# Out-projection of a three-branch flow step: token tiles in pairs, seven half-size products in place of eight

## The chip, the cores and the metric

The kernel runs on one core of a Trainium2 chip. The metric is device time in microseconds (us) of one launch. Engines are called as the profile calls them: PE (TensorE, matrix products), DVE (VectorE), ACT (ScalarE), POOL (GpSimd) and SP (SyncE, which issues most DMA transfers). PE writes its products to banks of PSUM; DVE and ACT read them there; POOL works on SBUF alone.

## What is computed

A layer of a flow model works on 2,048 sample tokens and 128 prompt tokens of width 1,024. An input projection feeds three token mixers; their outputs are projected, gated and summed into `merged`. What the change touches is the end:

```python
merged = jnp.einsum('btnd,btnd->btd', gt, pb)
out = jnp.einsum('btd,de->bte', merged, w_out)
h = h + gate * out
y = rmsnorm(h, final_g)
```

All tensors are float32. The kernel carries each operand of a large product as two float16 parts, hi and lo, and forms hi·hi + hi·lo + lo·hi, three products for one.

## The kernel before

The launch is one long program; a scheduler sets the order of the instructions on each engine by dependences and by priority (code under `tc.high_priority()` goes ahead of what could run beside it), and each engine then works strictly through its own list. The part before the change is the third merge (branch n = 0): `merge` goes through eight blocks `db` of 128 output columns. In each block PE forms, for five spans of tokens (four of 512 columns, one of 128), 24 products for the sigmoid gate (`gemm_T` with the kept input `xh`, `xl`) and 12 for the branch projection; ACT takes the sigmoid (L1389), DVE multiplies (L1398), POOL adds to the row `mrow` (L1399), and POOL's queue writes the row to the DRAM tensor `mrg` (L1406). The weights of later blocks are loaded to the two buffers `wst`, scaled and split beside this. In every block `tail` calls `out_w`, which loads one eighth of W_out, measures it and splits it into `whi`, `wlo` (names `wohi`, `wolo` in the trace).

The scale of a tensor comes from `scales` (L183 to L187): the sums of squares of 128 partitions are cast (L175), added up by a one-column product with a tile of ones on PE, and three short DVE operations turn the result into a power of two. The one-column product of an out-projection tile is the row `b<-mscb,ones`.

The out-projection goes through 17 tiles of 128 tokens, in the order 16 (the prompt), 8 to 15, 0 to 7. `out_prep` loads a tile of `mrg` (L1455), squares it on ACT (L1464), gets its scale, and splits it (L1466 on ACT for hi, L1467 on DVE for lo), all from L1464 on under high priority. It is called for the first five tiles before the last half of the last merge block (`ahead_out`), and then for tile i + 5 while tile i is worked on. PE forms 24 products of 128x512 for each half of the output (`gemm_N`). DVE multiplies with the gate (L1524), POOL adds the residual rows (L1525), ACT squares (L1534), DVE and POOL make the inverse root (L170, L171), DVE scales (L1537), and SP issues the store (L1538).

## Time and profile before

| | |
|---|---|
| median of 3 runs | 2188.82 us (2185.91 to 2192.23) |
| the profiled execution | 2189.41 us, span 2187.6 us |
| PE busy | 2123.6 us, 97% of the span |
| DVE, ACT, POOL busy | 60%, 46%, 32% |
| mean granted PE clock | 0.991 |
| last merge ends, last product of the out-projection | 2001.4, 2179.8 |

PE is the engine that sets the time; what matters of the others is where PE waits for them. In the views a time such as 2004.05 is microseconds from the start of the span. A row `x128` counts instructions; the mean of one product is longer than the distance between two, because products overlap in the array. In a view of stretches, PEclk is the granted clock as a share of full speed.

### The profile page before, as it was taken

What the parts mean: (1) busy time and instruction counts of PE and PEld (TensorE: products, weight loads), DVE (VectorE), ACT (ScalarE), POOL (GpSimd) and SP (SyncE); (2) the same over time, 40 slices, a digit from 0 to 9 for tenths busy, and PEclk for the clock granted to TensorE, in tenths of its full rate; (3) what the DMA queues carried; (4) which work ended last, traced back from release to release, by engine and by line L of the source; (5) the groups of instructions that cost most, each with busy time, mean ns of one, the idle gap of its engine ahead of it and who ended that gap; (6) DMA issues with size and microseconds to landing.
All of it is one profiled execution on the core that took longest, in us unless ns stands there. A gap on an engine that the chain in (4) does not pass through costs nothing.

```text
span 2187.6 us, 42676 instructions
## 1 busy us (share of the span) xinstructions
PE 2123.6 (97%) x16234; PEld 1214.9 (56%) x16234; DVE 1320.9 (60%) x3150; ACT 1015.0 (46%) x2355; POOL 701.6 (32%) x862
## 2 busy tenths in 40 slices
PE   7999999999999998999899999999999999999998
PEld 3565444455555587878555556555554444444443
DVE  5746854469879698776665555765663544323454
ACT  3644744345566474554544445655543422222332
POOL 1421333223334324322312223344432221222543
PEclk9999999999999999999999999999999999999999
DMA  8424823167777664544655555766654544324542
GB/s 282 141 87 148 290 95 106 61 204 222 253 232 240 198 197 139 146 121 127 197 183 157 174 160 180 242 196 203 198 173 150 174 129 129 116 78 127 173 148 103
DMA packets 304727, 365.09 MB, mean 167 GB/s; under 512 B 39585, under 2 KB 215946, under 8 KB 302474
## 3 DMA queue, kind: packets, MB, share of 16 engines
q1 hardware_dynamic: 289386, 302.19, 45.4%
q0 software_dynamic: 12688, 51.27, 6.5%
q10 hardware_dynamic: 2448, 8.91, 1.0%
q8 instruction: 127, 2.08, 0.4%
q14 instruction: 78, 0.64, 0.1%
HBM read 234.67 MB, written 127.62 MB: 166 GB/s over the span
## 4 chain that ended last, share of the span: by engine, by line
PE 50%; DMA 4%; DVE 4%; ACT 1%; issue 1%; POOL 0%; SPq 0%; DVEq 0%; POOLq 0%; ACTq 0%
PE b L161 50%; DMA st<-br 1%; DMA ES<-ei 1%; DMA mrg<-mrow 1%; DMA wst<-in_w_in_dram 0%; DVE XB L797 0%; DVE E L798 0%; DVE big L1360 0%; DMA mrow<-mrg 0%; DMA S<-in_state_delta_dram 0%; DMA wst<-in_w_branch_dram 0%; PE b L1057 0%; ACT big L1359 0%; DMA sq__2210_18514<-qT 0%; DMA qk<-n 0%
## 5 line engine op out<-in xcount | busy, mean ns | idle before, releaser
L161 PE MATMUL b<-xh,whi 128*128 128x512 f16 (+1 forms) x1920 | 652.6, 349 | 1.4 <-DVE mrow L1395 1.0
L161 PE MATMUL b<-xl,whi 128*128 128x512 f16 (+1 forms) x1920 | 652.9, 349 | 0.0
L161 PE MATMUL b<-xh,wlo 128*128 128x512 f16 (+1 forms) x1920 | 651.6, 348 | 0.0
L161 PEld LDWEIGHTS <-whi 128*128 128x128 f16 x3904 | 358.1, 98 | 329.2 <-issue 10.2
L161 PEld LDWEIGHTS <-wlo 128*128 128x128 f16 x1952 | 191.6, 98 | 179.0 <-issue 3.6
L161 PE MATMUL b<-big,bhi 128*128 128x512 f16 (+1 forms) x960 | 249.7, 347 | 1.4 <-ACT big L1359 1.1
L1399 POOL TENSOR_TENSOR mrow<-mrow,sg 128x512 f32<-128x512 f32 (+1 forms) x80 | 92.6, 1158 | 282.9 <-DVE sg L1398 220.5
L161 PE MATMUL b<-big,blo 128*128 128x512 f16 (+1 forms) x480 | 163.1, 347 | 0.0
L1389 ACT ACTIVATE sg<-b,winv 128x512 f32<-128x512 f32 (+1 forms) x120 | 74.2, 618 | 172.0 <-PE b L161 171.1
L161 PEld LDWEIGHTS <-xh 128*128 128x128 f16 x1496 | 117.7, 98 | 28.0
L161 PEld LDWEIGHTS <-bhi 128*128 128x128 f16 x960 | 86.9, 98 | 75.6
L1398 DVE SCALAR_TENSOR_TENSOR sg<-b,binv,sg 128x512 f32<-128x512 f32 (+1 forms) x80 | 53.4, 667 | 121.4 <-PE b L161 118.7
L646 POOL TENSOR_TENSOR cy<-cy,raw 128x545 f32<-128x545 f32 (+1 forms) x48 | 66.4, 1408 | 185.7 <-ACT raw L645 185.7
L175 DVE CAST wscb<-wss 128x1 bf16<-128x1 f32 x93 | 14.3, 154 | 154.5 <-ACT wlo L209 71.4
L866 POOL COPY T<-ES 32x256 f16<-32x256 f16 x68 | 31.0, 456 | 220.1 <-DMA ES<-ei 217.6
L161 PE MATMUL b<-whi,xh 128*128 128x128 f16 x544 | 94.0, 220 | 0.0
L161 PE MATMUL b<-wlo,xh 128*128 128x128 f16 x544 | 93.9, 220 | 0.0
L161 PE MATMUL b<-whi,xl 128*128 128x128 f16 x544 | 93.8, 220 | 0.0
L161 PE MATMUL b<-wohi,mh 128*128 128x512 f16 x240 | 90.9, 379 | 1.3 <-ACT mh L1466 1.3
L161 PE MATMUL b<-wohi,ml 128*128 128x512 f16 x240 | 90.8, 379 | 0.3 <-DVE mscb L175 0.3
L161 PE MATMUL b<-wolo,mh 128*128 128x512 f16 x240 | 90.9, 379 | 0.0
L209 ACT ACTIVATE wlo<-wst 128x1024 f16<-128x1024 f32 x52 | 54.9, 1056 | 77.4 <-DMA wst<-in_w_in_dram 75.5
(456 smaller groups left out, 4298.1 us busy)
## 6 DMA issues: line engine op xcount, KB each, us to landing
wst<-in_w_in_dram SPq DMA_DIRECT2D x60, 512.0 KB
qkv<-cy POOLq DMA_DIRECT2D x12, 1089.0 KB, 5.2
st<-br SPq DMA_DIRECT2D x48, 256.0 KB
mrow<-mrg SPq DMA_DIRECT2D x18, 512.0 KB
mrow<-mrg SPq DMA_DIRECT2D x16, 576.0 KB
mrg<-mrow POOLq DMA_DIRECT2D x16, 576.0 KB, 3.6
dc<-dec SPq DMA_DIRECT2D x17, 512.0 KB
kq<-qkv SPq DMA_DIRECT2D x34, 256.0 KB
```

What stands on the lines that cost most here:

```text
L161: PE.matmul(out, l, r, start=start, stop=stop)
L175: V.tensor_copy(sb16, ss)
L209: A.activation(w.lo, st, AF.Square, accum_out=ss)
L646: G.tensor_tensor(y[:, c0:c1], y[:, c0:c1], raw[:, 1 + c0:1 + c1], ALU.mult)
L866: G.tensor_copy(T16[rows(a0, b), :, :, b], ES[0:32, :, 2 * a0 + b, :, wT])
L1389: A.activation(sg, ps, AF.Sigmoid, scale=gw.inv)
L1398: V.scalar_tensor_tensor(sg, ps, binv[:, 1:2], sg, ALU.mult, ALU.mult)
L1399: G.tensor_tensor(mr, mr, sg, ALU.add)
```

## The change

The 16 sample tiles are taken in eight pairs. A pair of tiles (a above b) times W_out is a product of 2 x 2 blocks: four blocks of 128 tokens x 512 channels on one side and four quarters of W_out (512 x 512) on the other. Instead of eight block products the kernel forms seven, of sums and differences of the blocks (Strassen's scheme in the form with few additions). Tile 16 stays single.

- Four sums of W_out quarters are made in blocks 3 to 6 of the last merge (`out_pair`), split into hi and lo, and written to a DRAM tensor `tw` of 4.19 MB; after the merge they are loaded over `xh`, which has no reader left. All of W_out has one scale now, measured in blocks 0 to 2 (`out_squares`), so W_out is read twice.
- For each pair POOL makes four sums of the blocks of a and b (`pair_sums`), one scale is taken for both tiles (`m_scale`), and `pair_operands` splits seven operands, with ACT for hi and DVE for lo, into the place of `xl`. Only the splitting stands under high priority.
- Each product (`formed`) is 12 matrix products of 128x512 in one bank. The seven are joined by ACT copies (`kept`), DVE additions (`joined`) and POOL additions, then gated and added as before.
- The operands of pair i + 1 are prepared at the end of the code of pair i; only tile 16 and the sums of the first pair are prepared ahead.

```diff
+    def out_squares(i):
+        st = read_w(w_out[0][:, i * P:(i + 1) * P], KT)
+        A.activation(sb(orp, [P, KT, P], "t16", F16, bufs=2), st, AF.Square, accum_out=wos[:, i:i + 1])
+
+    def out_pair(j):
...
+        left, right = [read_w(w_out[0][:, i * P:(i + 1) * P], KT) for i in (j, j + 4)]
+        for i, st in ((j, left), (j + 4, right)):
+            hi, lo = [w_[:, :, i * P:(i + 1) * P] for w_ in (whi, wlo)]
+            A.activation(hi, st, AF.Copy, scale=s)
+            V.scalar_tensor_tensor(lo, st, s, hi, ALU.mult, ALU.subtract)
...
+            G.tensor_tensor(tf, x_, y_, op_)
+            t16 = sb(orp, [P, 2, 4, P], "t16", F16, bufs=2)
+            A.activation(t16[:, 0], tf, AF.Copy, scale=s)
+            V.scalar_tensor_tensor(t16[:, 1], tf, s, t16[:, 0], ALU.mult, ALU.subtract)
+            SY.dma_start(twD[:, n, j], t16.rearrange("p l k c -> p (l k c)"))
...
+    def m_scale(mts):
...
+            A.activation(jk, mt, AF.Square, accum_out=ss[:, i:i + 1])
...
+        s, inv = scales(ss[:, 2:3] if len(mts) > 1 else ss[:, 0:1], orp, "msc")
...
+    def pair_sums(ts, pl, tag):
+        a, b = [m_load(t, pl, tag) for t in ts]
+        s, minv = m_scale([a, b])
...
+        G.tensor_tensor(sf[:, 0], a21, a22, ALU.add)
+        G.tensor_tensor(sf[:, 1], sf[:, 0], a11, ALU.subtract)
+        G.tensor_tensor(sf[:, 2], a11, a21, ALU.subtract)
+        G.tensor_tensor(sf[:, 3], a12, sf[:, 1], ALU.subtract)
...
+        with tc.high_priority():
+            halved(v[:, 0, 0:2].rearrange("p s k c -> p (s k) c"), v[:, 1, 0:2].rearrange("p s k c -> p (s k) c"), a, s)
+            halved(v[:, 0, 2], v[:, 1, 2], b[:, 4:8], s)
+            halved(v[:, 0, 3:7], v[:, 1, 3:7], sf, s)
...
-            for i, t in enumerate(order[:5]):
-                pre.append(out_prep(t, *((wp, "wst") if i % 3 else (big, "mrow")), None if i < 3 else wp))
+            pre.append(out_single(16))
+            pre.append(pair_sums(PAIRS[0], wp, "wst"))
...
+    for n in (2, 0, 1, 3):
+        SY.dma_start(tw[:, n].rearrange("p j l k c -> p j (l k c)"), twD[:, n])
+    nxt = pair_operands(0, *pre[1])
...
+        def formed(slot, w, even):
+            ps = bank(ps_mm if even else ps_d, [P, 512])
+            for k in range(4):
+                mm(ps, v[:, 0, slot, k, :], w(0, k), k == 0, False)
+                mm(ps, v[:, 0, slot, k, :], w(1, k), False, False)
+                mm(ps, v[:, 1, slot, k, :], w(0, k), False, k == 3)
+            return ps
...
+        u1 = kept(formed(0, raw(0, 0), True))
+        u2 = joined(temp(), formed(4, mixed(2), False), u1)
+        c11 = joined(u1, formed(1, raw(1, 0), True), u1)
...
+        u5 = kept(formed(3, mixed(0), False))
+        u3 = joined(temp(), formed(5, mixed(1), True), u2)
+        G.tensor_tensor(u2, u2, u5, ALU.add)
+        G.tensor_tensor(u5, u3, u5, ALU.add)
...
+        c12 = joined(u2, formed(6, raw(1, 1), False), u2)
...
+        c21 = joined(u3, formed(2, mixed(3), True), u3)
...
+        if not end:
+            nxt = pair_operands(i_ + 1, *pair_sums(PAIRS[i_ + 1], op, "mt"))
```

Where the instructions stand is shown at three places. On PE before, in the middle of a tile of the out-projection (`wohi`, `wolo` are W_out, `mh`, `ml` the tile, `b` a PSUM bank, `mscb` the cast sums of squares of a tile five places later):

```order
L161 MATMUL b_26086<-wohi_23213,mh_25695 128x512
L161 LDWEIGHTS ones_2_89
L161 MATMUL b_25867<-mscb_25868,ones_2_89 128x1
L161 LDWEIGHTS mh_25695
L161 MATMUL b_26086<-wolo_23214,mh_25695 128x512
L161 LDWEIGHTS ml_25696
L161 MATMUL b_26086<-wohi_23213,ml_25696 128x512
```

On PE in the changed kernel, where the second pair ends and the third begins (`xh` holds the sums of W_out quarters, `xl` the seven operands; `b_25854` is the pair's last product, `mscb` belongs to the third pair, whose products begin with `b_25912` and `b_25942`):

```order
L161 MATMUL b_25854<-xh_93,xl_94 128x512
L161 LDWEIGHTS ones_2_89
L161 MATMUL b_25885<-mscb_25886,ones_2_89 128x1
L161 LDWEIGHTS xl_94
L161 MATMUL b_25912<-wohi_23213,xl_94 128x512
L161 LDWEIGHTS xl_94
L161 MATMUL b_25912<-wolo_23214,xl_94 128x512
L161 LDWEIGHTS xl_94
L161 MATMUL b_25942<-wohi_23213,xl_94 128x512
```

The one-column product has moved from between the products of other, earlier tiles to the seam between two pairs, directly ahead of the products that need its scale.

On DVE before, around the same one-column product `b_25867` (`inv` is the gate's factor, `ml` the lo part):

```order
L1524 TENSOR_TENSOR hh_26056<-b_26059,gt_26057 128x512
L183 COPY msc_25871<-b_25867 128x1
L185 TENSOR_SCALAR msc_25871<-msc_25871 128x1
L186 TENSOR_SCALAR msc_25871<-msc_25871 128x1
L187 TENSOR_SCALAR msc_25871<-msc_25871 128x1
L1469 TENSOR_SCALAR inv_3224_25878<-winv_2810_23215,msc_25871 128x8
L1467 SCALAR_TENSOR_TENSOR ml_25864<-mt_25861,msc_25871,mh_25863 128x1024
```

On DVE in the changed kernel, at the same seam (`sg_25813` is the block that the last product `b_25854` completes, `hss` the inverse root of the finished rows `hh`, `xl` the lo operands of the third pair, `sf` the sums that POOL made):

```order
L1631 TENSOR_TENSOR sg_25813<-b_25854,sg_25813 128x512
L183 COPY msc_25889<-b_25885 128x1
L1607 SCALAR_TENSOR_TENSOR sg_25813<-sg_25813,minv_25734,gb_25522 128x512
L185 TENSOR_SCALAR msc_25889<-msc_25889 128x1
L170 TENSOR_SCALAR hss_25848<-hss_25848 128x1
L186 TENSOR_SCALAR msc_25889<-msc_25889 128x1
L187 TENSOR_SCALAR msc_25889<-msc_25889 128x1
L1489 TENSOR_TENSOR minv_25894<-msc_25889,osc_24076 128x1
L1494 SCALAR_TENSOR_TENSOR xl_94<-mt_25876,msc_25889,xl_94 128x1024
L1577 SCALAR_TENSOR_TENSOR hh_25747<-hh_25747,hss_25848,fg_25524 128x1024
L1494 SCALAR_TENSOR_TENSOR xl_94<-mt_25878,msc_25889,xl_94 128x512
L1494 SCALAR_TENSOR_TENSOR xl_94<-sf_25896,msc_25889,xl_94 128x2048
```

The scale (L183 to L186) now stands among the operations that join and gate the last product, and the splitting follows it.

On SP in the changed kernel, at the end of the merge (`mrow` and `wst` from `mrg` with 8x128 are tile 16 and the first pair, `mt` the second pair; before, five tiles were loaded at this place and nothing as large as `tw`):

```order
L1477 DMA mrow_25369<-mrg 128x8x128
L1477 DMA wst_25389<-mrg 128x8x128
L1477 DMA wst_25391<-mrg 128x8x128
L1377 DMA mrow_25418<-mrg 128x1024
L1553 DMA xh_93<-tw 128x4096 x4
L1559 DMA hh_25520<-in_x_prompt_dram 128x1024
L1564 DMA gb_25522<-gate 128x1024
L1566 DMA fg_25524<-in_final_g_dram 128x1024
L1559 DMA hh_25587<-in_x_sample_dram 128x1024
L1559 DMA hh_25589<-in_x_sample_dram 128x1024
L1477 DMA mt_25716<-mrg 128x8x128
L1477 DMA mt_25718<-mrg 128x8x128
```

The four loads of `tw` stand ahead of the residual rows and of the second pair's tiles.

More of the change, by code (lines that the diff above doesn't have):

```diff
@@ L1507, in hybrid_flow_kernel @@
     SY.dma_start(fg, final_g[None, :].to_broadcast([P, D]))
[L1509 to L1529 removed]
+    jk = sb(op, [P, D], "ojk", F16, bufs=1)
```

160 lines of the change are left out of this document (105 added, 55 removed).

## Prediction

> **What bounds the kernel now.** I read the busy shares first, then the stretch of the out-projection, then the chain that ended last there, then the groups of the same stretch for durations.
>
> ```profile
> core 0: us, PE busy (x) PEld busy (x) DVE busy (x) ACT busy (x) POOL busy (x), PEclk, DMA share, GB/s
> 2004.00:2092.00 88.00, 87.97 (x415) 40.04 (x416) 45.00 (x94) 27.36 (x39) 44.02 (x36) 1.00 0.53 172
> ```
>
> ```profile
> 2004.05 175.78 PE b L161 x826
> ```
>
> PE has no gap in this stretch, its clock is full, and it carries the chain for 175.8 us. DVE, ACT and POOL are half idle or more. So products taken away are worth their full distance, and every moment in which PE waits costs its full length. The distance between two products is read from two starts, eleven apart:
>
> ```profile
> 2177.06 0.38 PE L161 MATMUL b<-wohi,mh 128*128 128x512 f16 x1
> ...
> 2179.43 0.38 PE L161 MATMUL b<-wohi,ml 128*128 128x512 f16 x1
> ```
>
> 2.37 us / 11 = 0.2155 us.
>
> **Products removed.** A pair had 2 x 48 products and has 7 x 12 = 84. Eight pairs save 96 x 0.2155 = **20.7 us**. Tile 16 is unchanged.
>
> **End of the merge.**
>
> ```profile
> 1998.19 1.06 ACT L1464 ACTIVATE ml<-wst 128x1024 f16<-128x1024 f32 x1 [0.71 <-DMA wst<-mrg]
> ...
> 1999.89 1.06 ACT L1464 ACTIVATE wlo<-mrow 128x1024 f16<-128x1024 f32 x1 [0.55 <-DMA mrow<-mrg]
> ...
> 2001.51 1.14 ACT L1466 ACTIVATE mh<-mrow,msc 128x1024 f16<-128x1024 f32 x1
> ...
> 2002.69 1.28 DVE L1467 SCALAR_TENSOR_TENSOR ml<-mrow,msc,mh 128x1024 f16<-128x1024 f32 x1 [0.23 <-ACT mh L1466]
> ```
>
> Before, tile 16's hi waits behind a fourth square that now isn't there (three tiles are loaded ahead, not five). Hi can start at 2000.1, after the third square and the last sigmoid (0.7), lo at 2001.3, and PE goes on at 2002.6, not 2004.05: **-1.4 us**. The first pair's operands: POOL's block sums and row additions from 1998.2 on (five by 1.27 us, row below) end at 2004.6, ACT's hi of 28 blocks of 128 columns (1.15 us for eight, as the row above) at 2007.9 and DVE's lo of the last 16 at 2010.5; PE has done tile 16 at 2002.6 + 44 x 0.2155 = 2012.1. So nothing waits there.
>
> **The seam between two pairs.** The durations (each row ends its first part with busy time and mean ns of one):
>
> ```profile
> L1525 POOL TENSOR_TENSOR hh<-hh,xr 128x512 f32<-128x512 f32 x30 | 38.0, 1267 | 74.0 <-DVE hh L1524 44.8 <-issue 24.6 <-DVE msc L187 4.5
> L1524 DVE TENSOR_TENSOR hh<-b,gt 128x512 f32<-128x512 f32 x32 | 22.0, 687 | 26.0 <-PE b L161 22.8 <-POOL gt L1489 3.0 <-DMA out_dram<-hh 0.2
> L1467 DVE SCALAR_TENSOR_TENSOR ml<-mt,msc,mh 128x1024 f16<-128x1024 f32 x12 | 15.4, 1283 | 3.0 <-ACT mh L1466 3.0
> L1464 ACT ACTIVATE ml<-mt 128x1024 f16<-128x1024 f32 x12 | 12.7, 1057 | 36.4 <-PE b L161 27.0 <-POOL hh L1525 7.4 <-DMA mt<-mrg 2.0
> L171 POOL TENSOR_TENSOR hss<-hss,mhalf 128x1 f32<-128x1 f32 x17 | 9.3, 550 | 1.8 <-DVE hss L170 1.8
> L1537 DVE SCALAR_TENSOR_TENSOR hh<-hh,hss,fg 128x512 f32<-128x512 f32 x2 | 1.4, 749 | 0.7 <-POOL hss L171 0.7
> ```
>
> The way from scale to hi, in order of time:
>
> ```profile
> 2004.20 0.15 DVE L185 TENSOR_SCALAR msc<-msc 128x1 int32<-128x1 int32 x1
> 2004.39 0.15 DVE L186 TENSOR_SCALAR msc<-msc 128x1 int32<-128x1 int32 x1
> ...
> 2004.57 1.15 ACT L1466 ACTIVATE mh<-wst,msc 128x1024 f16<-128x1024 f32 x1 [1.92 <-DVE msc L186]
> ```
>
> Preparing the next pair is not under high priority up to its scale, so PE's list has the one-column product behind the last product of the running pair, and the first products of the next pair right behind it. Nothing is left on PE to cover the way from scale to operands. From the end of the last product (0): DVE joins its bank (0.04 to 0.72), copies the scale (0.08 more until the next start), gates the block (L1607, two SBUF operands, as the 749 ns row: 0.82 to 1.57), then L185, a short L170 and L186 (1.57 to 1.91, the second start 0.19 after the first as in the rows); ACT splits tile a for hi (1.94 to 3.09). PE restarts at **3.1**. It can do four hi products (0.86), then waits for lo: DVE 3.13 to 4.41, PE at 4.48, another **0.5**. The other operands (hi by 6.1, lo by 9.0) are ready before PE reaches them at 8.8. L170 needs ACT's square of the finished rows, which needs POOL's addition (done 0.2 after the end, square 1.4): no further delay. So a seam costs **3.6 us** of waiting; bounds: 2.4 without the join and the gate in front of the scale, 4.6 if POOL slows a DVE operation by 1 us. That is for five seams. At the sixth of the seven, DVE's list has two gate operations between copy and L186: 4.5.
>
> The first seam is longer. The second pair's tiles are loaded behind `tw` and five transfers of 0.52 MB. Loads ran here at:
>
> ```profile
> 2016.00:2022.00 6.00, 6.00 (x29) 2.71 (x28) 2.08 (x6) 1.15 (x1) 2.22 (x2) 1.00 0.90 263
> ```
>
> Before, tiles of 0.524 MB landed 1.70 us apart at the merge's end (the two ACT rows above that waited for DMA), 308 GB/s. `tw` can start when PE has read `xh` for the last time, at 1999: 4.19 + 3.67 MB then take 30 us at 263 GB/s, 25.5 at 308, and the second tile lands at 2029 or 2025. (`tw` itself comes in time: its first quarter is there by 2004, and used at 2014.7.) The first pair's products end at 2012.1 + 84 x 0.2155 = 2030.2. From the landing on, POOL makes three block sums (ACT's two squares and `kept`, 2 x 1.06 + 0.7, end within them), a join, a sum and a join (6 x 1.27 = 7.6); DVE gates that result (0.75), joins the last block (0.69), and comes to L186 after 1.2 as above; ACT's hi takes 1.15: 11.4 us together. PE restarts at 2036.4 to 2040.4, 6.2 to 10.2 us late, and 0.5 for lo. I take **8**, between the two.
> Seams together: 5 x 3.6 + 4.5 + 8 = **30.5 us**.
> Inside a pair the change adds a wait on ACT: the square of the next pair's second tile stands ahead of the first `kept`. That tile's buffer comes free with DVE's lo at 4.4 and its load needs some 4 us (row under the merge's blocks); PE needs the bank that `kept` empties at the seventh product, 72 x 0.2155 = 15.5 us after its start. No cost.
>
> **PE's clock.** What did idle stretches of this size do to it? Pairs of rows: an idle stretch, then 3.4 us shortly behind it.
>
> ```profile
> 603.88:606.28 2.40, 0.00 (x0) 0.03 (x1) 2.31 (x5) 2.40 (x12) 0.45 (x1) 1.00 0.87 236
> 606.97:610.38 3.41, 3.41 (x13) 1.39 (x11) 3.38 (x9) 3.41 (x16) 2.94 (x3) 0.51 1.03 363
> 1056.88:1059.70 2.82, 0.00 (x1) 0.03 (x1) 1.61 (x6) 2.47 (x6) 1.03 (x2) 1.00 1.00 379
> 1060.99:1064.40 3.41, 3.33 (x39) 3.17 (x37) 3.24 (x11) 1.79 (x6) 0.15 (x1) 0.50 0.40 107
> 1539.90:1541.66 1.76, 0.00 (x1) 0.00 (x0) 0.38 (x4) 1.10 (x3) 0.00 (x0) 1.00 1.05 369
> 1542.27:1545.68 3.41, 3.27 (x16) 1.88 (x17) 2.90 (x7) 0.56 (x1) 0.26 (x1) 0.50 0.20 58
> 2001.40:2002.70 1.30, 0.01 (x2) 0.00 (x0) 0.83 (x3) 1.25 (x2) 0.41 (x1) 1.00 0.00 0
> 2002.70:2006.10 3.40, 3.11 (x15) 1.40 (x16) 2.41 (x8) 1.15 (x1) 0.00 (x0) 1.00 0.29 61
> ```
>
> ```profile
> 708.31:710.11 1.80, 0.01 (x1) 0.00 (x0) 1.80 (x3) 1.80 (x4) 0.00 (x0) 1.00 0.01 2
> 710.80:714.20 3.40, 2.97 (x49) 2.71 (x47) 3.40 (x11) 2.65 (x6) 2.93 (x4) 1.00 0.82 176
> ```
>
> Idle for 1.76, 2.40 and 2.82 us, then half clock for 3.41 us; idle for 1.30 and once for 1.80 us, no drop. Seams of 3.1 us are beyond all of these, so I count one half-clock stretch each, 3.41 / 2 = 1.7 us: 7 x 1.7 = **11.9 us** (bounds 0, and 23.8 for two each).
> [...]
>
> **The last merge's blocks.** Squares, splits and POOL sums cost nothing by themselves: 4 x 36 products of 0.2155 us and the short span cover 33 us in each block, and blocks 3 to 6 add some 6 us to each of ACT, DVE and POOL. But the next weights go to the same two buffers, and PE stands at their one-column products. A load takes 3.7 us to use, and L1398 takes 0.75:
>
> ```profile
> L1398 DVE SCALAR_TENSOR_TENSOR sg<-b,binv,sg 128x512 f32<-128x512 f32 x32 | 24.0, 750 | 101.9 <-PE b L161 99.4 <-ACT sg L1389 2.0 <-issue 0.3
> ```
>
> ```profile
> 1845.49 0.37 SPq L195 DMA_DIRECT2D wst<-in_w_out_dram  x1
> ...
> 1849.19 1.06 ACT L209 ACTIVATE wolo<-wst 128x1024 f16<-128x1024 f32 x1 [1.02 <-DMA wst<-in_w_out_dram]
> ```
>
> In block 4 the second W_out tile gets its buffer 3.4 us into the block and lands at 7.1; DVE ends that tile's lo at 9.5 (1.15 + 1.28) and L1398 at 10.3, POOL a row addition at 11.6 and its second sum at 12.9, which frees the buffer; the branch weights are there at 16.6 and measured and cast at 17.6. PE stands at their product after 72 long and 16 short products, at 16.4: 1.2 us late; by the same working 0.9 in block 5 and none in 3 and 6. I take **+2.0** (0 to 8: 2 us in each of the four), short enough to leave the clock.
>
> **The tail.**
>
> ```profile
> 2179.85 0.69 DVE L1524 TENSOR_TENSOR hh<-b,gt 128x512 f32<-128x512 f32 x1 [3.62 <-PE b L161]
> ...
> 2183.21 1.41 DVE L1537 SCALAR_TENSOR_TENSOR hh<-hh,hss,fg 128x512 f32<-128x512 f32 x2 [0.66 <-POOL hss L171]
> ```
>
> Before, the last scaling starts 3.4 us after the last product. Now DVE has two joins, two gates, a further gate and an addition of 0.7 each (to 3.9), then the other tile's full scaling, which waits for POOL's root (to 6.1), then sum, root (0.55) and scaling at 7.1: **+3.7 us**.
>
> **Sum:** -20.7 + 30.5 + 11.9 - 1.4 + 2.0 + 3.7 = **+26.0 us**. The profiled execution took 2189.41 us with a span of 2187.6, 0.6 above the median; on the median of 2188.8 the forecast is **2214.8 us**. A measurement can tell about 0.3% (6.6 us) from no change.
>
> **Rivals.**
> - *The clock stays full*: the four hi products inside each seam count as activity, and no drop follows. Everything else stands: 2214.8 - 11.9 = 2202.9 us. For it, the 1.80 us gap that had no drop; against it, three drops at gaps shorter than a seam. Chance 0.18. [...]
> - *Longer seams*: POOL, busy with sums at each seam, slows a DVE operation there (+1 us x 7), the first seam takes 11 (+3), all four merge blocks wait (+6): 2230.8 us. For it, one of DVE's scalings took a microsecond more than the others while POOL worked:
>
> ```profile
> 2042.85 2.28 DVE L1537 SCALAR_TENSOR_TENSOR hh<-hh,hss,fg 128x1024 f32<-128x1024 f32 x1 [0.41 <-POOL hss L171]
> ...
> 2052.41 1.28 DVE L1537 SCALAR_TENSOR_TENSOR hh<-hh,hss,fg 128x1024 f32<-128x1024 f32 x1 [1.03 <-POOL hss L171]
> ```
>
> Against it, most such rows show no increase. Chance 0.13.
> - *Short seams*: 2.4 us of waiting at six of them (14.4), 8 at the first, full clock: -20.7 + 22.4 - 1.4 + 2.0 + 3.7 = +6.0, 2194.8 us, no change. Chance 0.05.
> - *Faster: the one-column product runs early.* If PE took it while the pair's products run, the scale, hi and lo would be ready at the seam: six seams at 0, the first at 2: -20.7 + 2 - 1.4 + 2.0 + 3.7 = -14.4, 2174.4 us. The point from which it decides: -20.7 - 1.4 + 2.0 + 3.7 = -16.4, so seams that cost under 16.4 / 7 = 2.3 us each, clock included, make the kernel faster, under 1.4 us by more than 0.3%. Against it, DVE's cast below was ready to run at 1997.5 and waited for PE, which had not yet read the cast before it, since that product kept its place among the merge's products:
>
> ```profile
> 1997.30 0.19 ACT L1464 ACTIVATION_READ_ACCUMULATOR ml<-wst 128x1 f32 x1
> ...
> 1998.71 0.16 DVE L175 CAST mscb<-mss 128x1 bf16<-128x1 f32 x1 [2.85 <-PE b L161]
> ```
>
> Chance 0.06. That the change doesn't do what it says can be left aside: the order shows 84 products a pair.
>
> **How the numbers follow.** Forecast 0.58. The low end, 2198, is the full clock with no wait in the merge and a first seam of 6 (2202.9 - 2 - 2, rounded down); the high end, 2232, is the longer-seams case. Below lie short and early seams (0.11), above some of the rest. Slower by over 0.3% (above 2195.4): 0.58 + 0.18 + 0.13 = 0.89, less 0.02 for errors common to all cases, 0.87; within 0.3%: 0.05 and one of these, 0.06; faster: 0.07.
>
> **What would show it.** Right: in the new profile PE idles seven times, each time until ACT's hi (L1493) and then DVE's lo (L1494), 3 us and 0.5 us, with PEclk 0.5 behind each; products of the out-projection number 720; the last L1577 starts 7 us after the last product. Wrong: PE busy through the seams, or a drop of the clock at no seam, or PE waits of over 2 us in a merge block.

## The result, and the profile after

The changed kernel takes **2244.51 us** (median of 6 runs, 2242.13 to 2248.70), the kernel before 2188.61 us on the same chip (6 runs, 2185.91 to 2193.03): a ratio of 1.0253, 95% interval 1.0237 to 1.0268. The forecast was 2214.8 us, 2198 to 2232. The sign is right; the size is not, by 30 us, and the time lies outside the range. The profiled execution took 2242.51 us with a span of 2240.7.

I cut the span into four stages at instructions that all kernels here have: up to the one-column product ahead of the last merge's first block; the merge, up to the one-column product that stands directly behind its last product (that of the tile or pair after tile 16); the out-projection, up to the last product's end; the tail.

| us | start of the merge | merge | out-projection | tail | span |
|---|---|---|---|---|---|
| before | 1732.9 | 268.4 | 178.6 | 7.8 | 2187.6 |
| after | 1728.3 | 294.7 | 204.5 | 13.1 | 2240.7 |
| difference | -4.6 | **+26.3** | +26.0 | +5.3 | +53.1 |

The first stage is not touched by the change. It ended between 1726 and 1743 us in the 19 profiled executions of this study, so kernels that differ by a few us are compared by stage below, and only times of several runs by their medians.

The stretch of the merge, before and then after (columns as in the prediction: length, busy time of PE, PEld, DVE, ACT, POOL, granted clock, DMA share, GB/s):

```profile
1732.80:2001.20 268.40, 268.40 (x1473) 129.79 (x1473) 90.48 (x255) 70.12 (x115) 54.24 (x58) 1.00 0.36 112
```

```profile
1728.30:2023.10 294.80, 275.28 (x1468) 132.59 (x1467) 103.51 (x233) 80.61 (x129) 80.70 (x74) 0.97 0.42 132
...
2026.00:2114.00 88.00, 72.97 (x315) 31.36 (x314) 56.04 (x80) 33.55 (x46) 52.65 (x42) 0.92 0.54 183
```

The merge had no gap on PE before. Now PE is idle for 19.5 us in it and the clock is at 0.97. The last row answers to the stretch of the out-projection that the prediction starts from: 73 us of PE's work in 88 us, at 0.92 of the clock. What PE waited for (total us, times, longest), first over the whole kernel, the longest total, then in the merge (1728 to 2026 us):

```profile
PE b L161 <- ACT xl L1493: 32.1, 7, 7.5
```

```profile
PE b L161 <- DVE wscb L175: 12.2, 4, 5.8
PE b L161 <- ACT sg L1389: 4.5, 2, 3.9
PE b L161 <- DVE sg L1398: 2.8, 2, 2.0
```

The first row is the seven seams between pairs: 32.1 us, and the forecast said 30.5. The other three, 19.5 us together, hardly exist in the prediction. `wscb` is the scale of the next block's weights; the sigmoid (L1389) and the multiplication (L1398) empty PE's banks.

**A merge block.** Block 4 in order of time, on SP, ACT, DVE and PE (start, length, what; idle time before it and who ended it):

```profile
1874.14 0.38 SPq L195 DMA_DIRECT2D wst<-in_w_out_dram  x1
1874.79 0.39 PE L161 MATMUL b<-xh,whi 128*128 128x512 f16 x1
1877.78 1.15 ACT L1463 ACTIVATE wohi<-wst,osc 128x1024 f16<-128x1024 f32 x1 [5.28 <-DMA wst<-in_w_out_dram]
1878.96 1.28 DVE L1464 SCALAR_TENSOR_TENSOR wolo<-wst,osc,wohi 128x1024 f16<-128x1024 f32 x1 [4.85 <-ACT wohi L1463]
1882.76 1.28 DVE L223 SCALAR_TENSOR_TENSOR wlo<-wst,wsc,whi 128x1024 f16<-128x1024 f32 x1 [0.49 <-ACT whi L222]
1884.08 0.38 SPq L195 DMA_DIRECT2D wst<-in_w_out_dram  x1
1889.29 1.15 ACT L1463 ACTIVATE wohi<-wst,osc 128x1024 f16<-128x1024 f32 x1 [5.99 <-DMA wst<-in_w_out_dram]
1890.48 1.31 DVE L1464 SCALAR_TENSOR_TENSOR wolo<-wst,osc,wohi 128x1024 f16<-128x1024 f32 x1 [6.43 <-ACT wohi L1463]
1891.71 0.74 DVE L1398 SCALAR_TENSOR_TENSOR sg<-b,binv,sg 128x512 f32<-128x512 f32 x1
1892.50 0.22 PE L161 MATMUL b<-xh,whi 128*128 128x128 f16 x1 [2.00 <-DVE sg L1398]
1895.48 0.38 SPq L195 DMA_DIRECT2D wst<-in_w_branch_dram  x1
1899.14 0.16 DVE L175 CAST wscb<-wss 128x1 bf16<-128x1 f32 x1 [2.15 <-ACT blo L209]
1899.35 0.16 PE L161 MATMUL b<-wscb,ones 128*128 128x1 bf16 x1 [5.79 <-DVE wscb L175]
```

Read it from the second W_out load (1884.08). It is issued 9.3 us into the block, because its buffer is freed by DVE's `wlo` (1882.76), which waits for ACT, whose list held the split of the first W_out tile ahead of it and stood 5.28 us at that tile's transfer. The second tile makes ACT and DVE stand again (5.99 and 6.43 us), and L1398, which only has to empty a bank, stands in DVE's list behind that tile's lo: PE idles 2.00 us. The branch weights get a buffer at 1895.48, and PE idles 5.79 us at their scale. The same in block 1 with the squares: ACT stood 6.67 us at a tile to be squared, with a sigmoid behind it, and PE idled 3.86.

**The clock.** Idle stretches and the half clock behind them, in the merge and at a seam:

```profile
1893.55:1899.36 5.81, 0.02 (x2) 0.01 (x1) 0.97 (x3) 2.27 (x5) 3.16 (x3) 0.56 0.39 135
1894.24:1904.48 10.24, 5.13 (x29) 3.21 (x29) 5.29 (x14) 4.44 (x8) 6.38 (x6) 0.50 0.29 98
...
2081.17:2084.90 3.73, 0.00 (x1) 0.00 (x1) 2.11 (x9) 2.35 (x4) 3.73 (x3) 1.00 0.00 0
2085.39:2088.80 3.41, 3.41 (x9) 0.94 (x8) 2.97 (x4) 3.00 (x4) 1.24 (x1) 0.50 0.37 104
```

In the merge the clock was half for 17.1 us, 5.3 of them while PE stood anyway: half of the rest, 5.9 us, is lost, since products started 0.426 us apart at 0.50 of the clock (1788.43 to 1791.41) and 0.2155 at full. In the out-projection it was half for 30.7 us, 4.4 of them idle: 13.1 lost.

**A seam**, the second one:

```profile
2081.01 0.17 PE L161 MATMUL b<-mscb,ones 128*128 128x1 bf16 x1
2081.21 0.69 DVE L1631 TENSOR_TENSOR sg<-b,sg 128x512 f32<-128x512 f32 x1
2081.82 0.15 DVE L183 COPY msc<-b 128x1 f32<-128x1 f32 x1
2081.93 0.85 DVE L1607 SCALAR_TENSOR_TENSOR sg<-sg,minv,gb 128x512 f32<-128x512 f32 x1
2082.27 1.06 ACT L1572 ACTIVATE ojk<-hh 128x1024 f16<-128x1024 f32 x1 [7.38 <-POOL hh L1610]
...
2083.45 0.15 DVE L170 TENSOR_SCALAR hss<-hss 128x1 f32<-128x1 f32 x1 [0.60 <-ACT ojk L1572]
2083.52 0.14 DVE L186 TENSOR_SCALAR msc<-msc 128x1 int32<-128x1 int32 x1
...
2083.70 1.76 ACT L1493 ACTIVATE xl<-mt,msc 128x1024 f16<-128x1024 f32 x2 [0.28 <-DVE msc L186]
...
2084.90 0.39 PE L161 MATMUL b<-wohi,xl 128*128 128x512 f16 x1 [3.73 <-ACT xl L1493]
```

The order is the one forecast: one-column product last, join, scale, gate, the scale's last step, hi. One wait was denied in the prediction and is there: L170 stands 0.60 us at ACT's square of finished rows.

**The tail**, on DVE, from PE's last product on:

```profile
2227.25 0.69 DVE L1631 TENSOR_TENSOR sg<-b,sg 128x512 f32<-128x512 f32 x1 [1.54 <-PE b L161]
2227.98 1.72 DVE L1607 SCALAR_TENSOR_TENSOR sg<-sg,minv,gb 128x512 f32<-128x512 f32 x2
...
2230.33 1.03 DVE L1607 SCALAR_TENSOR_TENSOR sg<-sg,minv,gb 128x512 f32<-128x512 f32 x1
2231.40 1.64 DVE L1610 TENSOR_TENSOR hh<-sg,hh 128x512 f32<-128x512 f32 x1
...
2235.97 1.41 DVE L1577 SCALAR_TENSOR_TENSOR hh<-hh,hss,fg 128x512 f32<-128x512 f32 x2 [0.66 <-POOL hss L171]
```

The last scaling starts 8.4 us after PE's end; 7.1 was forecast.

### The profile page after: what moved, and what is told of

Its sections match the earlier page's. It is cut to its first block, busy times and chain, and to the rows that moved or that the text cites. A ratio compares the mean times of both kernels' runs of the same rounds, so it can differ in the third digit from the quotient of the medians.

```text
span 2240.7 us, 42539 instructions
## 1 busy us (share of the span) xinstructions
PE 2118.0 (95%) x16123; PEld 1208.8 (54%) x16123; DVE 1371.2 (61%) x3124; ACT 1043.5 (47%) x2395; POOL 784.0 (35%) x908
## 5 line engine op out<-in xcount | busy, mean ns | idle before, releaser
L161 PEld LDWEIGHTS <-whi 128*128 128x128 f16 x3840 | 352.2, 98 | 330.2 <-issue 18.1
L161 PEld LDWEIGHTS <-xl 128*128 128x128 f16 x1488 | 141.5, 100 | 137.6 <-ACT xl L1493 34.1
L1399 POOL TENSOR_TENSOR mrow<-mrow,sg 128x512 f32<-128x512 f32 (+1 forms) x80 | 98.0, 1225 | 252.7 <-DVE sg L1398 183.5
L1389 ACT ACTIVATE sg<-b,winv 128x512 f32<-128x512 f32 (+1 forms) x120 | 74.0, 617 | 139.1 <-PE b L161 138.4
L646 POOL TENSOR_TENSOR cy<-cy,raw 128x545 f32<-128x545 f32 (+1 forms) x48 | 75.3, 1596 | 181.2 <-ACT raw L645 181.2
L1398 DVE SCALAR_TENSOR_TENSOR sg<-b,binv,sg 128x512 f32<-128x512 f32 (+1 forms) x80 | 53.3, 666 | 104.1 <-PE b L161 96.6
L161 PE MATMUL b<-wohi,xl 128*128 128x512 f16 x192 | 68.6, 428 | 32.7 <-ACT xl L1493 32.1
L175 DVE CAST wscb<-wss 128x1 bf16<-128x1 f32 x85 | 13.0, 153 | 134.7 <-ACT wlo L209 81.0
L223 DVE SCALAR_TENSOR_TENSOR wlo<-wst,wsc,whi 128x1024 f16<-128x1024 f32 x52 | 71.5, 1379 | 32.2 <-ACT whi L222 32.1
```

Source lines behind the costliest of these rows:

```text
L161: PE.matmul(out, l, r, start=start, stop=stop)
L175: V.tensor_copy(sb16, ss)
L223: V.scalar_tensor_tensor(w.lo, st, s, w.hi, ALU.mult, ALU.subtract)
L646: G.tensor_tensor(y[:, c0:c1], y[:, c0:c1], raw[:, 1 + c0:1 + c1], ALU.mult)
L1389: A.activation(sg, ps, AF.Sigmoid, scale=gw.inv)
L1398: V.scalar_tensor_tensor(sg, ps, binv[:, 1:2], sg, ALU.mult, ALU.mult)
```

## The experiments

Stages of each version, one profiled execution each (medians of several runs stand in the text where there are any; nosq, nosum, calm0, seam4, held, noadd and final2 ran once):

| us | start of the merge | merge | out-projection | tail | span |
|---|---|---|---|---|---|
| mergeonly | 1732.8 | 294.9 | 181.6 | 7.8 | 2217.2 |
| nosq | 1732.3 | 285.6 | 205.4 | 13.1 | 2236.4 |
| nosum | 1731.8 | 281.2 | 206.0 | 13.5 | 2232.6 |
| own | 1738.8 | 276.1 | 206.8 | 13.1 | 2234.8 |
| calm | 1736.8 | 267.9 | 204.4 | 10.6 | 2219.8 |
| calm0 | 1737.7 | 268.3 | 204.5 | 10.7 | 2221.1 |
| fill | 1735.7 | 292.9 | 198.9 | 13.1 | 2240.6 |
| seam | 1739.8 | 295.4 | 183.7 | 11.4 | 2230.2 |
| seam4 | 1736.2 | 293.4 | 180.1 | 15.2 | 2224.9 |
| held | 1737.9 | 296.2 | 170.3 | 13.3 | 2217.7 |
| noadd | 1735.2 | 296.7 | 177.5 | 9.6 | 2219.0 |
| best | 1742.8 | 278.1 | 179.9 | 18.1 | 2218.9 |
| final | 1735.7 | 269.5 | 170.2 | 13.4 | 2188.7 |
| final2 | 1734.7 | 267.9 | 169.5 | 16.4 | 2188.5 |
| final3 | 1733.8 | 267.9 | 172.0 | 15.8 | 2189.5 |
| final4 | 1738.7 | 267.9 | 170.1 | 14.4 | 2191.1 |
| final5 | 1725.7 | 268.3 | 178.4 | 13.2 | 2185.5 |

### The merge

**mergeonly**: the new merge with the out-projection of before (its `out_w` replaced by the two functions of the change, as they are).

```diff
-    def out_w(i):
-        w = load_w(w_out[0][:, i * P:(i + 1) * P], KT, hi=whi[:, :, i * P:(i + 1) * P], lo=wlo[:, :, i * P:(i + 1) * P])
...
+    def out_squares(i):
...
+    def out_pair(j):
...
+            V.tensor_copy(winv, wsc[1].to_broadcast([P, KT]))
```

> The changed kernel's last merge (one scale, squares, splits, quarter sums and their stores) with the out-projection of before (17 single tiles, eight products of quarters; the stored sums are not read). Theory A, the loss sits in the merge's blocks: the merge again takes some 294 us instead of 268, all behind it as before, 2188.6 + 26.4 = 2215 us (2208 to 2220). Rival B, the merge is late only because of the new preparation at its end (two tiles and pair sums instead of five tiles), or the loss sits in the out-projection: within 6 us of before, 2183 to 2195.

Measured: 2223.07 us (2218.97 to 2227.16, 2 runs) beside 2189.28 before; merge 294.9 us. The merge's 26 us are there without the pairs, and all of them: theory A, though the total lies 3 us above its range. (The out-projection takes 3 us more than before: PE waits 2.7 us for tile 16's hi part, with a half clock behind it.)

**nosq** and **nosum** take one kind of added work out of the merge.

```diff
 (nosq)
-            for i in range(3 * db, min(3 * db + 3, KT)):
-                out_squares(i)
+            if db == 0:
+                V.memset(wos[:, 0:KT], 1.0)
```

> The changed kernel without the eight squares of W_out's tiles and their eight loads in the first three blocks of the merge; the scale comes from a constant that gives the same power of two. Theory A (each wait in the merge belongs to one kind of tile in flight): PE's waits in the second block (2.3 and 3.9 us) and the half clock behind them (3.4 us, 1.7 lost) go, and those of the later blocks (12 us, 6.8 lost) stay: the merge takes 294.7 - 8 = 287 us (284 to 290). Rival B, waits only move: without the squares the later blocks wait longer, merge 292 us or more. Whole kernel about 2237 us.

```diff
 (nosum)
-            G.tensor_tensor(tf, x_, y_, op_)
-            t16 = sb(orp, [P, 2, 4, P], "t16", F16, bufs=2)
...
+        for n in range(4):
+            SY.dma_start(twD[:, n, j], zero)
```

> The changed kernel with the four quarter sums of each pair of W_out tiles and their splits left out (zeros are stored in their place, so the products with them are wrong); squares, loads and splits of W_out stay on the two shared buffers. Theory A (a W_out tile's buffer is late because of the in-order lists at its loads and splits): about half of the waits in blocks 4 to 6 (12 us and 6.8 us of clock) stay, since the second W_out tile is still loaded late and the next weights behind it; merge 294.7 - 8 = 287 us (282 to 291). Rival B, POOL's sums alone hold the buffers: the waits from block 4 on all go, merge 294.7 - 19 = 276 us or less.

Measured: without the squares 285.6 us (9.1 less), without the sums 281.2 (13.5 less). PE's idle stretches of block 1 went with the squares (11.7 us are left of 19.5), as theory A says for nosq. nosum lies between its two theories, outside both ranges and a little nearer to B (276) than to A (287): the sums hold the buffers for a good part, not alone. The two gains add up to 22.6 of the 26.3 us. Neither settles whether it is the work or the waiting for tiles.

**own**: the same work, W_out's tiles in a buffer that the merge's weights don't use.

```diff
+    LOADS = [(0, 1), (2, 3), (4, 5), (6, 7)] + [(j, j + 4) for j in range(4)]
+    def read_two():
+        st = sb(orp, [P, 4, 4, P], "sf").rearrange("p s k c -> p (s k) c")
...
-        left, right = [read_w(w_out[0][:, i * P:(i + 1) * P], KT) for i in (j, j + 4)]
+        left, right = two
```

> The changed kernel with W_out's tiles staged in the buffer of the pair sums, which is not yet in use, two tiles at a time and one pair of tiles ahead, instead of in the two buffers that the merge's weights use. Theory A, the merge loses its 26.4 us because W_out's tiles and the merge's weights wait for each other in two shared buffers, and ACT's and DVE's lists stand behind a tile in flight: PE's idle stretches of over 0.6 us in the merge go and with them the half clock, 2244.5 - 26 = 2218 us (2213 to 2224). Rival B, ACT, DVE and POOL are too busy with the added squares, splits and sums, whatever the buffers: at least 2235 us.

Measured: merge 276.1 us, so 18.6 of the 26.3 us go with a buffer of its own and the earlier loads that it allows; 2237.50 us (2236.59 to 2238.42, 2 runs) in all, which by its total is rival B. By its merge it is nearer to A: in the profiled execution the merge began late (1738.8). Some 4 us of that are the edit's own: ahead of the merge ACT stands 3.3 us at the first W_out tile and 3.2 us at a tile of the next weights, a sigmoid stands behind, and PE idles 2.1 us for it, with a half clock after; the rest lies within the spread of the start. What is left in the merge are two idle stretches of 2.9 and 2.8 us. The first is again a list that stands at a tile:

```profile
1877.52 1.01 SPq L1458 DMA_DIRECT2D sf<-in_w_out_dram  x2
...
1882.76 1.29 DVE L1476 SCALAR_TENSOR_TENSOR wolo<-sf,osc,wohi 128x1024 f16<-128x1024 f32 x1 [2.92 <-ACT wohi L1475]
...
1884.62 1.63 DVE L1476 SCALAR_TENSOR_TENSOR wolo<-sf,osc,wohi 128x1024 f16<-128x1024 f32 x1
1886.17 0.20 DVE L175 CAST wscb<-wss 128x1 bf16<-128x1 f32 x2
```

The tiles are asked for only when the last sums have freed the buffer, DVE's lo stands at them, and the cast (L175) that PE waits for comes behind both tiles' lo. The second stretch has another cause: L1398, at 1899.22, stands behind the lo of a sum of W_out quarters, which waits 2.13 us for ACT, and ACT waits 3.29 us for POOL's sum; the four sums of a tile pair go through one buffer (`tf`).

**calm** and **calm0**: the same splits, sums and stores, but a scale for each pair of column tiles (8 loads in place of 16), the separate buffer, and the four pairs spread over blocks 1, 3, 5 and 6; in calm they are also held back by a value of the running block.

```diff
+    def out_pair(j, one):
+        left, right = two
+        for i, st in enumerate(two):
+            A.activation(sb(orp, [P, KT, P], "t16", F16, bufs=2), st, AF.Square, scale=one, accum_out=wos[:, i:i + 1])
...
+        if j < 3:
+            read_two(j + 1)
...
+            one = sb(orp, [P, 1], "one")
+            V.tensor_scalar(one, sg[:, 0:1], 0.0, 1.0, ALU.mult, ALU.add)
```

> The changed kernel with another preparation of W_out: one scale for each pair of column tiles instead of one for all (so no squares ahead: 8 tile loads, not 16; the scales' inverses go into the gate rows), the pair of tiles staged in the pair sums' buffer, its load a block or more ahead, and its squares, splits and sums held back by a value of the running block's first sigmoid, so that ACT and DVE never stand at a tile in flight. The same splits, sums and stores as in the changed kernel. Theory A, the merge's 26 us come from lists that stand at tiles in flight, not from the work: merge 268.4 + 0 to 6 us (after: 294.7), whole kernel 2244.5 - 23 = 2221 us (2217 to 2227). Rival B, the added work by itself crowds ACT, DVE and POOL: merge 280 us or more.

```diff
 (calm0, against calm)
-            A.activation(sb(orp, [P, KT, P], "t16", F16, bufs=2), st, AF.Square, scale=one, accum_out=wos[:, i:i + 1])
+            A.activation(sb(orp, [P, KT, P], "t16", F16, bufs=2), st, AF.Square, accum_out=wos[:, i:i + 1])
```

> As the kernel whose merge lost nothing (267.9 us; one scale for each pair of column tiles, own staging buffer, held back by a value of the block's first sigmoid), but not held back: squares, splits and sums stand where the scheduler puts them, right behind the loads. Theory A, what cost the time is that ACT's and DVE's lists stand at tiles in flight: PE waits again in the merge, 274 us or more. Rival B, the eight loads left out and the separate buffer are enough: merge 272 us or less, as with the hold.

Measured: calm 2217.86 us (2214.14 to 2221.58, 2 runs), merge 267.9 us; calm0 268.3. The merge's stretch in calm:

```profile
1736.90:2004.90 268.00, 268.00 (x1471) 129.89 (x1470) 104.03 (x252) 84.15 (x140) 82.91 (x73) 1.00 0.41 129
```

Set it beside after's row: DVE, ACT and POOL do as much work (104.03, 84.15 and 82.91 us; after 103.51, 80.61 and 80.70), PE has no gap, the clock is full, and all 26.3 us are gone. So the work itself costs nothing; rival B is out. But my narrower theory is out too: without the holding back nothing comes back. In calm0 ACT did stand at W_out's tiles in the merge, and PE had no gap:

```profile
ACT t L1464 <- DMA sf<-in_w_out_dram: 15.6, 6, 3.5
```

In calm ACT stood at none, in the changed kernel 35.4 us (18.3 at tiles to be split, 17.1 at tiles to be squared), but in the kernel before, too, 17.6 us, six times, without a gap on PE. So a list that stands at a tile is not by itself the cost; it is where the buffer of the next weights, or the emptying of a bank, comes too late by it. What is shown is that the cost hangs on where the tiles are staged and how often they are loaded (own: 18.6 us by the buffer and its earlier loads; the rest goes with the halved loads and the wider spacing, which I did not take apart).

### The clock and the seams

**fill**: unused products in the seams.

```diff
-            nxt = pair_operands(i_ + 1, *pair_sums(PAIRS[i_ + 1], op, "mt"))
+            ab = pair_sums(PAIRS[i_ + 1], op, "mt")
+            ps = bank(ps_x, [P, 512])
+            for _ in range({0: 30, 5: 20}.get(i_, 12)):
+                mm(ps, v[:, 0, 2, 0, :], whi[:, 0, 0:512])
+            nxt = pair_operands(i_ + 1, *ab)
```

> The changed kernel with products that nothing uses put in each seam behind the one-column product: 12 of 128x512 (2.6 us), 30 in the first seam, 20 in the sixth; they end before the next pair's operands are ready, so no seam gets longer. Theory A, the half clock comes from PE's idle stretch at the seam: idle stretches of about 1.1 us stay, the clock stays full, 2244.5 - 13.6 = 2231 us (2228 to 2235). Rival B, the clock falls for another reason (what the other engines do there) and stays low: 2244 us, or a little more.

Measured: 2243.62 us (2242.38 to 2244.87, 2 runs), by its total rival B. The stages say otherwise: this execution's merge began 7.4 us later than after's, and the out-projection took 5.6 us less. Half clock in it fell from 30.7 to 6.8 us, and what is left stands where the filling was too short (columns as above):

```profile
2065.77:2066.95 1.18, 0.01 (x1) 0.00 (x1) 1.03 (x3) 1.18 (x2) 1.18 (x2) 1.00 0.00 0
2067.00:2070.40 3.40, 3.12 (x14) 1.25 (x15) 3.40 (x4) 3.40 (x4) 0.32 (x1) 1.00 0.19 46
2110.77:2113.74 2.97, 0.01 (x1) 0.00 (x1) 2.47 (x7) 2.25 (x4) 2.97 (x3) 1.00 0.00 0
2114.60:2118.01 3.41, 2.72 (x7) 0.89 (x7) 3.41 (x4) 2.63 (x3) 1.26 (x1) 0.50 0.29 78
```

Behind 1.18 us of idle time the clock stayed at 1.00, behind 2.97 it went to 0.50. Where the filling shortened the idle stretch, the half clock went (theory A). The gain is smaller than forecast because two seams became 1.8 us longer, and it is behind these two, idle for 2.97 and 2.96 us, that the half clock is left.

**seam** and **seam4**: the next pair is prepared in the middle of the running one; seam4 with a fourth tile buffer and earlier loads.

```diff
+        if not end:
+            nxt = pair_operands(i_ + 1, *pair_sums(*mts))
...
         u5 = kept(formed(3, mixed(0), False))
...
-        if not end:
-            nxt = pair_operands(i_ + 1, *pair_sums(PAIRS[i_ + 1], op, "mt"))
 (seam4)
-        mt = sb(pl, [P, KT, P], tag, bufs=3 if tag == "mt" else 2)
+        mt = sb(pl, [P, KT, P], tag, bufs=4 if tag == "mt" else 2)
```

> The changed kernel with the next pair's tiles loaded a pair ahead and its scale, sums and operands put behind the third of the running pair's seven products; the merge is not changed. Theory A, the seams cost their waits of 32.1 us and the half clock behind them of 13.6 us, and four products (10.3 us) cover the preparation: 2244.5 - 45.7 = 2199 us (2195 to 2206). Rival B, POOL and DVE have no room inside a pair (about 13.8 us each of 18.1), so that joins and gates come late and half of the waits come back at other places: 2215 to 2230 us.

> As the kernel with the next pair's preparation behind the third product, but with four instead of three buffers for the tiles of the merged rows, and the loads for the pair after the next put at a pair's start. There ACT waited 40 us for tiles of the next pair, and PE 11.8 us for the one-column product and 5.5 us for operands. Theory A, those waits come from tiles that are loaded too late: ACT's wait goes to under 5 us, PE's idle stretches of the out-projection from 17.3 to under 5 us, out-projection from the merge's end to PE's end 183.7 - 17 = 167 us (164 to 172), whole kernel about 2208 us. Rival B, they come from DVE and POOL being in each other's way (the gate took 1.19 us instead of 0.75, a POOL sum 2.6 instead of 1.27): out-projection 178 us or more.

Measured: seam 2226.67 us (2221.36 to 2231.98, 2 runs), out-projection 183.7; seam4 2226.70 us (1 run), 180.1. The preparation now has its cover, and 21 to 24 of the 45.7 us go; the rest comes back elsewhere, as rival B said. In seam PE waits 11.8 us for the one-column product; in seam4 it no longer does, but waits 15.9 us for operands. seam4 doesn't test theory A, since ACT still stands 34.4 us at tiles of the next pair (40.0 in seam).

**held** and **noadd** take POOL out of the way, each in another place.

```diff
 (held)
-        u5 = kept(formed(3, mixed(0), False))
-        G.tensor_tensor(u2, u2, u5, ALU.add)
-        G.tensor_tensor(u5, u3, u5, ALU.add)
+        p5 = formed(3, mixed(0), False)
+        u2 = joined(u2, p5, u2)
+        c22 = joined(temp(), p5, u3)
 (noadd)
-        gated(c11, c11, L)
-        added(ha, c11, L)
+        gated(ha[:, L], c11, L)
```

> As the kernel with four tile buffers and the preparation in the middle of a pair (out-projection 180.2 us there), but POOL's two joins of a pair (2.6 and 1.4 us) and ACT's copy of that product are replaced by two joins of DVE that read the product from its PSUM bank. Theory B (DVE and POOL in each other's way bound the out-projection), POOL has 4 us less in each pair and DVE 1.4 more: out-projection 170 to 176 us. Theory A (the waits come from the order of the lists and the tiles' loads): no change, 178 to 182 us.

> As the kernel with four tile buffers and the preparation in the middle of a pair, without the additions of the row block x (POOL's four of each pair, DVE's one at the end; the gate writes to the rows instead), so the output lacks that term. POOL has 5 to 6 us less in each pair. Theory B (POOL bounds the out-projection, and it slows DVE's gates and scalings): DVE's gate falls from 1.19 us to under 0.9, PE's waits from 16 us to under 6, out-projection 180.2 - 14 = 166 us (163 to 171). Theory A (the order of the lists): 176 us or more.

Measured: held 170.3 us, noadd 177.5 (seam4 180.1). The out-projection's stretch in seam4, held and noadd:

```profile
2029.60:2209.70 180.10, 162.13 (x729) 69.63 (x727) 140.83 (x183) 71.21 (x100) 131.70 (x94) 0.98 0.47 163
```

```profile
2034.10:2204.40 170.30, 158.52 (x729) 69.36 (x727) 145.58 (x199) 67.34 (x92) 99.18 (x80) 1.00 0.50 173
```

```profile
2031.70:2209.20 177.50, 161.08 (x730) 69.56 (x728) 135.01 (x186) 71.21 (x100) 92.26 (x67) 0.99 0.49 166
```

noadd spares POOL more (92.26 us) than held does (99.18), and DVE too, and yet gains 2.7 us against 9.8. DVE's gate didn't get faster either: 1202 ns in noadd and 1315 in held, 1231 in seam4. So POOL's load is not the bound, and theory B in that form falls, though held's number lies in its range. Nor are the tiles' loads worth these 9.8 us: ACT stands 33.6 us at them in held too. PE's waits for hi, from 2040 to 2200 us, in seam4, held and noadd:

```profile
PE b L161 <- ACT xl L1493: 6.5, 4, 2.7
```

```profile
PE b L161 <- ACT xl L1493: 0.8, 2, 0.4
```

```profile
PE b L161 <- ACT xl L1493: 5.8, 5, 1.5
```

Its waits for lo stay between 8.3 and 9.4 us. So most of held's gain is the waits for hi and the half clock behind idle stretches (3.1 us lost in seam4, none in held). What held alone takes away on DVE is the waiting for POOL's joins; in noadd it is still there:

```profile
DVE sg L1633 <- POOL sg L1645: 8.0, 7, 1.2
```

L1633 is DVE's join. Each of these 7 waits comes right behind the last lo half of a preparation, six of them ahead of the next pair's scale in DVE's list; that they make the scale, and with it hi, late is argued from this order, not shown. held also forms and adds the blocks of a pair in another order, which I didn't separate.

### Can the scheme gain?

**best**, **final**, **final2**, **final3**, **final4** and **final5** put the edits together (best also takes the last pair's products in another order; of final2 to final4 only some lines are shown).

```diff
 (best: own, seam4, and)
+            with tc.high_priority():
+                out_pair(db - 3)
 (final: calm and held)
 (final2, final3: last pair in the order 0, 4, 3, 1, 6, 5, 2; final3 also)
-            corner(u1, formed(1, raw(1, 0), True), u1, ha, L)
             nxt = prepared()
+            corner(u1, formed(1, raw(1, 0), True), u1, ha, L)
 (final4: final2, and in the last pair)
+            V.tensor_add(roots[:, 1:2], part[:, 0:1], part[:, 1:2])
+            rsqrt(roots, roots, 1.0 / D, 2)
 (final5: final4, and for the first tile of a pair)
-                V.scalar_tensor_tensor(hh[:, cs], hh[:, cs], ss2, fg[:, cs], ALU.mult, ALU.mult)
+                A.activation(hh[:, cs], hh[:, cs], AF.Copy, scale=ss2)
+                G.tensor_tensor(hh[:, cs], hh[:, cs], fg[:, cs], ALU.mult)
```

> Four edits of the changed kernel together: W_out's tiles staged in the pair sums' buffer one pair ahead, their splits and sums at high priority; the next pair's preparation in the middle of the running pair; four tile buffers; and in the last pair the first tile's rows are finished before the last two products. If the merge's waits go (268 + 5 us), the out-projection takes 167 us and the tail 10: 1733 + 273 + 167 + 10 = 2183 us (2176 to 2195), at or a little under before's 2189. Rival, merge waits of 8 us and DVE and POOL in each other's way in the out-projection stay: 2200 us or more.

Measured: 2218.21 us (2215.68 to 2220.74, 2 runs). The rival: merge 278.1, out-projection 179.9, and a tail of 18.1.

> The edits together: W_out prepared with a scale for each pair of tiles, held back and staged apart; four tile buffers; the next pair prepared in the middle of the running one; the two joins on DVE from PSUM. By the parts: 1733 + 271 for the merge + 174 for the out-projection + 11 for the tail = 2189 us, as before (2182 to 2198). Below before by more than 0.3% (under 2182) only if the merge shows no wait and the out-projection falls to 170 us.

Measured: 2188.27 us (2181.47 to 2193.74, 8 runs), before 2190.29 on that chip (9 runs); ratio 0.9991, 0.9974 to 1.0007. Level, as the parts add up.

> The kernel with all edits (out-projection 170.2 us, tail 13.4 us), with another order in the last pair: the first tile's rows are finished after the fifth product, so that only one block is left for DVE behind the last product. Theory A, the tail is DVE's backlog of joins and gates (from 2175.3 to 2180.5, against 2.1 us for one block): tail 13.4 - 4 = 9.4 us (8.5 to 10.5), whole kernel 2184 us (2179 to 2189 with the spread of the start). Rival B, POOL's root and the last store set it whatever the order: 12 us or more.

> As final2, and the next pair is prepared behind the second product of a pair instead of the third. Theory A, what is left in the out-projection (PE waits 8.9 us for DVE's operand halves, ten times) comes from the preparation ending when PE is already there; one product earlier (2.6 us) covers all but the first two: out-projection 170.2 - 6 = 164 us (161 to 167), whole kernel 2178 us (2173 to 2184), 0.5% under before's 2190. Rival B, DVE then does the joins later and PE waits for banks instead: out-projection 169 us or more, 2184 us or more.

Measured: final2 2190.29 us (1 run), tail 16.4; final3 2191.37 us (2185.84 to 2193.87, 10 runs), ratio 1.0001, 0.9984 to 1.0018, out-projection 172.0. Both missed, and both numbers are the rivals'. In final2 DVE's list reaches the last join only at 2179.34, 7 us after PE's end, because the first tile's root and scaling stand ahead of it (1.17 us of waiting for ACT's square, 0.44 for POOL's root, 2.28 for the scaling). In final3 PE waits 11.8 us for operand halves, not less than final2's 8.6; the waits for banks that its rival named are one of 1.0 us.

> As final2 (out-projection 169.5 us, tail 16.1 us), but in the last pair the two tiles' roots are taken together behind the last block, so that DVE's list no longer stands at the first tile's root (2176.0 to 2179.3) ahead of the last join. Theory A, that stand was the tail's excess: tail 16.1 - 3 = 13 us (11.5 to 14), whole kernel 2187 us (2182 to 2191). Rival B, another wait takes its place (POOL's additions beside DVE's gates): tail 15 us or more.

> As final4, and the first tile of each pair is scaled by ACT (root) and POOL (row of factors) instead of DVE. Theory A, DVE's list sets what is left of the out-projection's waits (8.6 us for operand halves): DVE has 1.3 to 1.6 us less in each pair, PE's waits fall by half, out-projection 169.5 - 4 = 165.5 us (162 to 168), whole kernel 2182 us (2177 to 2187), 0.3% under before. Rival B, POOL's 2.5 us more in each pair slow DVE's gates as much: 169 us or more, no better than final4.

Measured: final4 **2187.06 us** (2179.78 to 2192.98, 10 runs) beside 2190.22 before (2184.87 to 2196.51, 19 runs), ratio 0.9975, 0.996 to 0.9991; final5 2195.73 us (2187.32 to 2200.24, 10 runs), ratio 1.0024, 1.0011 to 1.0037. final4 is the only version whose interval lies under before, by a quarter of a per cent, less than the 0.3% that I named as the bound; it is the best of six, and its interval overlaps final's. Its total is theory A's; its tail, 14.4 us, lies between the two theories. Its merge and out-projection:

```profile
1738.80:2006.70 267.90, 267.90 (x1470) 129.85 (x1470) 101.92 (x250) 84.01 (x140) 83.59 (x73) 1.00 0.41 129
2006.70:2176.80 170.10, 159.75 (x729) 69.91 (x727) 138.97 (x196) 68.96 (x95) 98.30 (x80) 0.99 0.50 172
```

DVE is busy for 139 of 170 us here (before: 45 of 88). Of the 20.7 us of products the out-projection keeps 8.5 (178.6 - 170.1), and the tail gives back 6.5. final5 moved 1.3 us a pair from DVE to ACT and POOL and lost 8.3 us of the out-projection (178.4): POOL's busy time there rose from 98.30 to 122.07 us, and DVE's did not fall (140.55), as its rival B said.

## Why the prediction was wrong

Term by term, forecast and measured:

| us | forecast | measured |
|---|---|---|
| products | -20.7 | -20.7 (96 fewer, 0.2155 apart at full clock, in both profiles) |
| end of the merge | -1.4 | -0.3 |
| seams | +30.5 | +32.1 |
| clock behind the seams | +11.9 | +13.1 |
| **the last merge's blocks** | **+2.0** (0 to 8) | **+26.3** |
| tail | +3.7 | +5.3 |
| start of the merge | 0 | -4.6, run to run |
| sum | +26.0 | +51.2 of 53.1 |

The rest of 1.9 us is for 0.5 us short waits for lo behind three seams and, as an estimate, for 7 x (0.38 - 0.2155) = 1.2 us the end of the last product of each pair, which no next product overlaps any more.

**The step that failed** is "The last merge's blocks": "In block 4 the second W_out tile gets its buffer 3.4 us into the block and lands at 7.1". It got it at 9.3 and ACT had it at 14.5 (1889.29 - 1874.79). I had let each buffer come free when the work on it could be done. The two buffers are freed by ACT, DVE and POOL's sums, and ACT and DVE were both standing at the W_out tile loaded before; that is, the delay of one tile is the delay of the next buffer, and so of the next tile. The same rule was in my own text for PE ("the next weights go to the same two buffers"), and I worked it through for one pass of the ring only. L1398 and the sigmoids, which free PE's banks, stand in the same lists; I priced them as late by their own durations. The words "short enough to leave the clock" failed with it: 5.9 of the 26.3 us are the clock. And blocks 0 to 2, which I passed over because a square is cheap, cost 9.1 us (nosq). mergeonly shows the term alone, calm shows that it is not the work; how the 26.3 us divide between the shared buffers, the doubled loads and their spacing stays open.

**What held.** The one-column product has no cover, and PE stands seven times at ACT's hi. Four seams cost 3.7 us (forecast 3.6), the first 7.5 (8), the sixth 5.6 (4.5: besides the two gates a join stands there) and the last 4.1. That 3.6 came out is in part luck, since two errors cancel: hi came 3.7 us after the last product and not 3.1, as L170 stood at ACT's square for 0.6, which the prediction excluded; and the wait of 0.5 us for lo was 0.3 at most. The gates took up to 1.86 us rather than 0.75 (in the last seam, while POOL worked), which was part of the rival of longer seams. Each of the seven seams was followed by half clock, as the rows of the kernel before let expect; the rival with a full clock is refuted by the row of 2085.39. Shorter gaps were followed by half clock, too: 2.40 and 2.82 us in the kernel before, 2.97 us in fill.

The end of the merge: tile 16's first product came 0.7 us after the one-column product that ends the merge, 1.5 before. But hi had begun 0.5 us ahead of that product, where the forecast had 1.1, and lo took 1.80 us rather than 1.28, so that PE ran through only from 2.5 us on (2.8 before). The tail is DVE's backlog as forecast, with a gate of 1.03 us and an addition of 1.64 us, both while POOL worked, where the forecast had 0.7 each.

## What to carry to other kernels

A buffer ring that two streams share is priced by walking it round: when each buffer is freed, by whose list, and what that list stands at; an operation that waits for a transfer delays everything behind it on its engine, the short ones that free PSUM banks first of all (here L1398, behind a lo part that stood for 6.43 us: PE idled 2.00 us). Whether that costs anything is settled by what hangs behind: such waits of ACT, 17.6 us before and 15.6 in calm0, left no gap on PE. Before a scheme that saves products is tried, ask what each saved product costs on the engines beside PE: here 20.7 us of products could be turned into about 3 us, while DVE went from half busy to over 80% in that stage. And the new work cost nothing with 8 loads staged apart and spread over the time there is, where 16 loads through the shared buffers cost 26 us.
